# Weights that stand still in TensorE: two units worked off together, all upper products first

## The chip, the cores and the metric

The kernel runs on one core of one Trainium2 chip. What counts is the device time of one execution in microseconds (us), the median of several runs. Beside it there is one profiled execution, whose trace gives the begin and end of every instruction on every engine. The engines are TensorE (PE; its weight loads are shown apart as PEld), VectorE (DVE), ScalarE (ACT), GpSimd (POOL) and SyncE (SP), which issues most transfers (DMA) from the chip's memory.

## The reference

The program is a decoder trunk of two layers over one sequence of 256 positions, width 1024, in float32. Each layer is a feed-forward block (FFN), a mixer (a recurrent block in layer one, an attention in layer two), and a second FFN. Before layer two, keys and values are computed once.

```
def swiglu(x, w_gate, w_up, w_down):
    return (jax.nn.silu(x @ w_gate) * (x @ w_up)) @ w_down
...
    for layer in range(DEPTH):
        if layer == N_A_LAYERS:
            k, v, c = shared_kv(h, kv_norm_g, w_kv, w_fgate, b_fgate)
        f = swiglu(rms_norm(h, ffn1_pre_g[layer]), ffn1_w_gate[layer], ffn1_w_up[layer], ffn1_w_down[layer])
        h = h + 0.5 * rms_norm(f, ffn1_post_g[layer])
        ...  (mixer)
        f = swiglu(rms_norm(h, ffn2_pre_g[layer]), ffn2_w_gate[layer], ffn2_w_up[layer], ffn2_w_down[layer])
        h = h + 0.5 * rms_norm(f, ffn2_post_g[layer])
```

`w_gate` and `w_up` are 1024 x 2816, `w_down` is 2816 x 1024. There are four FFNs, so most of the weights, and most of the time, are theirs.

## The kernel before, in words

**Precision.** A float32 product is made of three products of a narrower type (fp32r). Every weight and every input is split into an upper part (rounded to fp32r) and a lower part (what is left). Upper weight times upper input, upper weight times lower input, and lower weight times upper input are added up in PSUM.

**Units.** Weights come in units of half a megabyte: 128 partitions of 1024 numbers. A unit is loaded into a tile `raw` (five buffers, by SP's queue), then ACT rounds it into `whi` (line 204) and DVE subtracts to get `wlo` (line 205); there are nine buffers of each (`WB`). The list `items` holds, in the order of use, a pair of functions for each unit: `prep` (load and split) and `work` (the products).

**Two ways to multiply.** For `w_down` and some others the input stands still in TensorE and the weights move through it (`mm3`, lines 212 to 214, products of 512 columns). For most of gate, up and the keys the weights stand still (`still`, line 518, and `mmj`, line 227). There a unit is two rows of 128 of the weight (k and k+1) by 512 columns, that is, eight blocks of 128 x 128. For each block, line 238 loads the upper weights and moves 512 columns through: the 256 upper inputs and the 256 lower inputs side by side. After these eight products, line 242 loads the lower weights and moves the 256 upper inputs only, again eight products. I call the first "upper products" and the second "lower products". Four units make a group (k from 0 to 7), which fills four of the eight PSUM banks; the next group uses the other four while ACT and DVE empty the first (line 513 adds up on ACT, line 514 on DVE, then lines 600, 601, 607, 611, 612 make the hidden values).

**Order.** PE's order is the order in which the program is written; the other engines' order is set by a scheduler from what is written. `slot` runs the next unit's `work`, counts the unit as done, and calls `tick`. `tick` is where other work is asked for: it counts down deferred functions (`defer`: transposes on PE, for instance) and runs those that are due, and it may call `prepare_next`, which asks for one more unit to be loaded and split if a model of the pace says so and the unit nine places back is done. `still` itself also calls `tick` once, after all sixteen products of the unit. So there are two ticks for each unit, both after the unit's lower products.

**The opening.** The first three units are worked off in halves, with other steps between (`hooks`: functions that bring up the next parts of the input, line 1350). Two ticks after the last of them is set, `rstd_rows` (line 298) is due: two small products on line 301 turn the row statistics into a row (`rrow`, copied out by ACT, line 303), which the first group's line 600 multiplies with. Its PSUM bank is one of those that the second group will use.

Of the kernel before, what the change touches and what calls it, by code (L numbers as in the profile page):

```python
# [16 lines left out]
P = 128  # L17
# [30 lines left out]
def trunk_kernel(ctx: ExitStack, tc: tile.TileContext, A: dict, out: bass.AP):  # L48
# [64 lines left out]
    def tick():  # L113
        for p in list(pend):
            p[0] -= 1
            if p[0] < 0 and not (p[2] and state["edge"]):
                pend.remove(p)
                p[1]()
        purse[0] = min(purse[0] + SHARE, SHARE)
        if state["p"] >= OPEN:  # L120
            prepare_next()
        while queue and purse[0] > 0:
            cost, _, fn = queue.pop(0)
            purse[0] -= cost
            fn()
# [101 lines left out]
    def mmj(bs, parts, ks, moving):  # L227

        o, oh = pall, pall[:, :, :S]
        if len(moving(ks[0])[0].shape) == 4:  # L230
            o = o.rearrange("p n (a t b) -> p n a t b", a=2, t=2)
            oh = oh.rearrange("p n (t b) -> p n t b", t=2)
        else:
            o = o.rearrange("p n (a b) -> p n a b", a=2)
        for k, (wh, wl) in zip(ks, parts):
            tensor_work(2 * S * len(bs))
            for b, w in zip(bs, wh):
                nc.tensor.matmul(o[:, b], w, moving(k)[0], start=k == 0, stop=False)  # L238
        for k, (wh, wl) in zip(ks, parts):
            tensor_work(S * len(bs))  # L240
            for b, w in zip(bs, wl):
                nc.tensor.matmul(oh[:, b], w, moving(k)[1], start=False, stop=k == 7)  # L242


    def rstd_of(ss, n, f=1.0):
# [128 lines left out]
    items = []  # L374
    units = {}
    done = {}
    state = {"p": 0, "a": 0, "b": 0, "edge": False, "look": 99}
# [23 lines left out]
    def slot(t, i):  # L401
        while state["p"] <= i:
            prepare_next(True)
        items[i][1](t, units[i])
        done[i] = done.get(i, 0) + (1 if t is not None else 2)
        if done[i] == 2:
            units.pop(i)
        tick()
# [106 lines left out]

    hooks = {}

    def still(u, k0, b0, moving=x_moving):
        if k0 == 0:
            assert not set(held) & set(range(b0, b0 + 4)), held.keys()  # L520
            lent.update(range(b0, b0 + 4))
        state["edge"] = k0 in (0, 6)
        parts = []
        for j in range(2):
            cut = [slice(j * 512 + b * P, j * 512 + b * P + P) for b in range(4)]
            parts.append(([u.hi[:, c] for c in cut], [u.lo[:, c] for c in cut]))
        if hooks:
            for j in range(2):
                if k0 + j in hooks:
                    hooks.pop(k0 + j)()  # L530
                mmj(range(b0, b0 + 4), parts[j:j + 1], [k0 + j], moving)
                if j == 0:
                    tick()
        else:
            mmj(range(b0, b0 + 4), parts, [k0, k0 + 1], moving)
            tick()
        if k0 == 6:
            lent.difference_update(range(b0, b0 + 4))
            state["edge"] = True

    def tile_items(w, c0, b0, post, moving=x_moving):
        for k0 in range(0, 8, 2):
            def prep(k0=k0):
                return split(load_raw(w[k0 * P:(k0 + 2) * P, c0:c0 + 512].rearrange("(k p) n -> p k n", p=P), P, 1024),
                             P, 1024)

            def work(t, u, k0=k0):
                still(u, k0, b0, moving)
                if k0 == 6:
                    post(b0, 4)  # L550
            items.append((prep, work))

    def ffn_items(pool_of, wg, wu, wd, post_g, next_dests, last=False, normed=False, lead=1):
        hid = {}
        sil = {}
        box = {}

        def hid_tiles():
            if not hid:
                v = hid["all"] = pool_of().tile([P, 2, 2, 22, P], F32R, tag="hid", name=nm("hid"), bufs=1)  # L560
                hid["hhi"], hid["hlo"] = v[:, 0], v[:, 1]
            return hid["hhi"], hid["hlo"]

        def gate_tile(n):
            return pool_of().tile([P, 1024], F32, tag="sil", name=nm("sil"), bufs=1)[:, :n]

        def prod_tile(n):
            return pool_of().tile([P, 16 * HA], F32, tag="prod", name=nm("prod"), bufs=1)[:, :n]

        def post_gate(t, ps):  # L570
            if t == 0:
                box["s"] = gate_tile(1024)
            s = sil[t] = box["s"][:, t * 512:(t + 1) * 512]
            nc.scalar.activation(s, ps, AF.Silu, scale=rs[t][:, 0:1])

        def post_up(c0):
            def f(t, ps):
                if t == 0:
                    box["p"] = prod_tile(1024)
                pr = box["p"][:, t * 512:(t + 1) * 512]  # L580
                nc.vector.tensor_tensor(pr, ps, sil[t], ALU.mult)
                defer(HT, lambda: hidden_T(pr, t))

            def hidden_T(pr, t):
                hh, hl = hid_tiles()
                tp = sparebank()
                for j in range(4):
                    nc.tensor.transpose(tp[:, j * P:(j + 1) * P], pr[:, j * P:(j + 1) * P], ident)
                k0 = c0 // P
                hv = hh[:, t, k0:k0 + 4, :].rearrange("p a b -> p (a b)")  # L590
                lv = hl[:, t, k0:k0 + 4, :].rearrange("p a b -> p (a b)")
                nc.scalar.activation(hv, tp, AF.Copy)
                nc.vector.tensor_tensor(lv, tp, hv.bitcast(F32), ALU.subtract)
            return f

        def gate_rows(b, m):
            s = sil["j"] = gate_tile(m * S)
            v = s.rearrange("p (a b) -> p a b", a=m)
            total(v, b, m)
            nc.vector.tensor_tensor(v, v, rcp["v"].unsqueeze(1).to_broadcast([P, m, S]), ALU.mult)  # L600
            nc.scalar.activation(s, s, AF.Silu)  # L601

        def up_rows(b, m, k0):
            pr = prod_tile(m * S)
            hh, hl = hid_tiles()
            total(pr.rearrange("p (a b) -> p a b", a=m), b, m)
            nc.vector.tensor_tensor(pr, pr, sil["j"], ALU.mult)  # L607
            pv = pr.rearrange("p (a t b) -> p a t b", a=m, t=2)
            hv = hh[:, :, k0:k0 + m, :].rearrange("p t a b -> p a t b")
            lv = hl[:, :, k0:k0 + m, :].rearrange("p t a b -> p a t b")  # L610
            nc.scalar.activation(hv, pv, AF.Copy)  # L611
            nc.vector.tensor_tensor(lv, pv, hv.bitcast(F32), ALU.subtract)

        def last_items(c0):
            for k0 in range(0, 8, 2):
                def prep(k0=k0):
                    raw = new_raw()
                    v = raw.rearrange("p (k s n) -> p k s n", k=2, s=2)
                    for s, w in enumerate((wg, wu)):
                        nc.sync.dma_start(v[:, :, s, :], w[k0 * P:(k0 + 2) * P, c0:c0 + 256].rearrange("(k p) n -> p k n", p=P))  # L620
                    return split(raw, P, 1024)

                def work(t, u, k0=k0):
                    still(u, k0, 4)
                    if k0 == 6:
                        gate_rows(4, 2)
                        up_rows(6, 2, c0 // P)
                items.append((prep, work))

        i0 = len(items)  # L630
        for i in range(5):
            if i < lead:
                proj_items(wg, i * 512, 512, main_x, post_gate)
                proj_items(wu, i * 512, 512, main_x, post_up(i * 512))
            else:
                tile_items(wg, i * 512, 4, gate_rows)
                tile_items(wu, i * 512, 0, lambda b, m, i=i: up_rows(b, m, 4 * i))
        last_items(2560)

        def load_gb():  # L640
            box["gb"] = gain_bcast(post_g)

        ahead(i0 + 24, load_gb)

        def post_down(t, accs):
            enter(t, next_dests(t, hid), accs, box["gb"], True, last, normed)

        i2 = len(items)
        row_items(wd, [P] * 22, lambda t, k: (hid["hhi"][:, t, k, :], hid["hlo"][:, t, k, :]), post_down, 4 if last else 2)
        return i0 + 8 * lead, i2, len(items)  # L650
# [625 lines left out]
    for i in range(OPEN):  # L1276
        u = units[i] = Unit()
# [165 lines left out]
```

## Time and profile before

| what | value |
|---|---|
| median of three runs | 991.96 us (991.91 to 992.14) |
| profiled execution, its own time | 991.76 us |
| its span (first to last instruction of the program) | 990.0 us |
| PE busy, PEld busy | 978.2 us, 836.3 us |
| DVE busy, ACT busy | 675.8 us, 564.2 us |
| moved from memory | 182.06 MB, 184 GB/s over the span |
| granted TensorE clock | 0.999 |

A row of the page's list of groups reads: line, engine, operation, what is written from what, shapes and count; after the bar, busy time and the mean of one in nanoseconds; after the second bar, how long the engine sat idle before such an instruction and who ended most of that. A matmul's shown time covers its whole passage through the array, and successive ones overlap, so that what a product costs is the distance from its start to the next one's start. A row of the timeline gives start and length in us, engine, line, operation, and how many instructions in a row it merges; an idle time before it stands in brackets with what ended it.

### The profile page before, as it was taken

How to read it: one execution, taken by the hardware profiler on the slowest of the kernel's cores; microseconds unless marked ns; L12 is line 12 of the kernel's file. 1: busy time of each engine (PE TensorE's matmuls, PEld its weight loads, DVE VectorE, ACT ScalarE, POOL GpSimd, SP SyncE). 2: the span in 40 equal slices, each digit the busy share in tenths (PEclk: the TensorE clock that was granted, in tenths of full speed). 3: DMA queues.
4: the chain of work that ended last, by engine and by line, in shares of the span. 5: the costliest groups of instructions: out<-in, count | busy, mean ns of one | idle time of the engine just before them, and what ended most of it. 6: DMA issues, size and time to landing. Idle time of an engine off the chain costs nothing.

```text
span 990.0 us, 13894 instructions
## 1 busy us (share of the span) xinstructions
PE 978.2 (99%) x5294; PEld 836.3 (84%) x5294; DVE 675.8 (68%) x791; ACT 564.2 (57%) x740; POOL 51.4 (5%) x97
## 2 busy tenths in 40 slices
PE   8999999999999999999999999999999999999997
PEld 6888888899978888888898888888887688888885
DVE  5877664668997776664697676674488867667542
ACT  6666543559986655543565555553467666555431
POOL 3300000100003000000000000000030000000000
PEclk9999999999999999999999999999999999999999
DMA  7887645565337766646468666654585157665431
GB/s 259 267 281 223 199 150 191 167 182 154 113 101 233 235 191 186 196 150 179 116 217 280 190 182 192 194 189 157 171 296 173 40 174 246 190 194 187 154 116 42
DMA packets 94088, 182.06 MB, mean 184 GB/s; under 512 B 11822, under 2 KB 33414, under 8 KB 93894
## 3 DMA queue, kind: packets, MB, share of 16 engines
q1 hardware_dynamic: 93350, 181.10, 58.7%
q8 instruction: 41, 0.67, 0.3%
q0 software_dynamic: 640, 0.07, 0.1%
q14 instruction: 25, 0.20, 0.1%
q10 hardware_dynamic: 32, 0.01, 0.0%
HBM read 180.09 MB, written 1.06 MB: 183 GB/s over the span
## 4 chain that ended last, share of the span: by engine, by line
PE 72%; issue 21%; DVE 3%; ACT 3%; POOL 1%; DMA 0%; DVEq 0%; POOLq 0%; SPq 0%; ACTq 0%
PE pall L238 25%; PE pall L242 13%; PE pall L212 9%; PE pall L214 9%; PE pall L213 9%; PE pall L865 1%; PE pall L219 1%; PE pall L220 1%; PE pall L221 1%; DVE wlo L205 1%; PE pall L1169 1%; PE pall L1196 1%; POOL rstd L250 1%; ACT whi L204 0%; ACT junk L255 0%
## 5 line engine op out<-in xcount | busy, mean ns | idle before, releaser
L205 DVE TENSOR_TENSOR wlo<-raw,whi 128x1024 fp32r<-128x1024 f32 (+4 forms) x328 | 393.1, 1206 | 237.5 <-ACT whi L204 236.2
L204 ACT ACTIVATE whi<-raw 128x1024 fp32r<-128x1024 f32 (+4 forms) x328 | 340.7, 1046 | 286.3 <-PE pall L214 114.4
L238 PE MATMUL pall<-xall,whi 128*128 128x512 f32 x1280 | 321.9, 393 | 1.4 <-ACT rrow L303 0.9
L238 PEld LDWEIGHTS pall<-xall,whi 128*128 128x128 f32 x1280 | 230.0, 189 | 43.2 <-ACT rrow L303 1.1
L242 PEld LDWEIGHTS pall<-xall,wlo 128*128 128x128 f32 x1280 | 174.9, 190 | 13.1 <-DVE wlo L1301 0.4
L242 PE MATMUL pall<-xall,wlo 128*128 128x256 f32 x1280 | 179.0, 282 | 0.0
L212 PE MATMUL pall<-whi,hid 128*128 128x512 f32 (+2 forms) x400 | 153.0, 382 | 0.0
L214 PE MATMUL pall<-whi,hid 128*128 128x512 f32 (+2 forms) x400 | 152.4, 381 | 0.3 <-DVE hid L278 0.3
L213 PE MATMUL pall<-wlo,hid 128*128 128x512 f32 (+2 forms) x400 | 152.4, 381 | 0.0
L214 PEld LDWEIGHTS pall<-whi,hid 128*128 128x128 f32 x400 | 75.1, 188 | 14.3 <-DVE hid L278 0.6
L213 PEld LDWEIGHTS pall<-wlo,hid 128*128 128x128 f32 x400 | 75.1, 188 | 13.6
L212 PEld LDWEIGHTS pall<-whi,hid 128*128 128x128 f32 x400 | 75.1, 188 | 13.6
L248 POOL TENSOR_SCALAR nv<-ss 128x1 f32<-128x1 f32 x24 | 10.4, 435 | 926.1 <-ACT junk L255 925.9
L212 PE MATMUL pall<-whi,xall 128*128 128x512 f32 (+2 forms) x144 | 57.2, 397 | 0.0
L214 PE MATMUL pall<-whi,xall 128*128 128x512 f32 (+2 forms) x144 | 55.2, 383 | 0.0
L213 PE MATMUL pall<-wlo,xall 128*128 128x512 f32 (+2 forms) x144 | 55.0, 382 | 0.0
L601 ACT ACTIVATE sil<-sil 128x1024 f32<-128x1024 f32 (+1 forms) x22 | 21.6, 984 | 24.7 <-DVE sil L600 24.7
L611 ACT ACTIVATE hid<-prod 128x1024 fp32r<-128x1024 f32 (+1 forms) x22 | 21.6, 984 | 19.3 <-DVE prod L607 19.3
L214 PEld LDWEIGHTS pall<-whi,xall 128*128 128x128 f32 x144 | 27.0, 188 | 5.4 <-DVE xall L278 0.3
L212 PEld LDWEIGHTS pall<-whi,xall 128*128 128x128 f32 x144 | 27.1, 188 | 4.9
L213 PEld LDWEIGHTS pall<-wlo,xall 128*128 128x128 f32 x144 | 27.1, 188 | 4.5
L318 DVE SCALAR_TENSOR_TENSOR t<-pall,rstd,gb 128x512 f32<-128x512 f32 x16 | 11.9, 748 | 26.7 <-ACT junk L255 26.7
(193 smaller groups left out, 978.7 us busy)
## 6 DMA issues: line engine op xcount, KB each, us to landing
raw<-in_ffn_w_down_dram SPq DMA_DIRECT2D x88, 512.0 KB
raw<-in_ffn_w_up_dram SPq DMA_DIRECT2D x80, 512.0 KB
raw<-in_ffn_w_gate_dram SPq DMA_DIRECT2D x78, 512.0 KB
raw<-in_rg_w_in_dram SPq DMA_DIRECT2D x20, 504.0 KB
raw<-in_ffn_w_gate_dram SPq DMA_DIRECT2D x20, 256.0 KB
raw<-in_rg_w_out_dram SPq DMA_DIRECT2D x10, 504.0 KB
raw<-in_ffn_w_up_dram SPq DMA_DIRECT2D x16, 256.0 KB
raw<-in_w_kv_dram SPq DMA_DIRECT2D x8, 512.0 KB
```

Source lines behind the costliest of these rows:

```text
L204: nc.scalar.activation(hi[:parts, c:c + m], rawv[:, c:c + m], AF.Copy)
L205: nc.vector.tensor_tensor(lo[:parts, c:c + m], rawv[:, c:c + m], hi[:parts, c:c + m].bitcast(F32), ALU.subtract)
L212: nc.tensor.matmul(ps, xh, wh, start=first, stop=False)
L213: nc.tensor.matmul(ps, xh, wl, start=False, stop=False)
L214: nc.tensor.matmul(ps, xl, wh, start=False, stop=last)
L219: nc.tensor.matmul(ps, wh, xh, start=first, stop=False)
L238: nc.tensor.matmul(o[:, b], w, moving(k)[0], start=k == 0, stop=False)
L242: nc.tensor.matmul(oh[:, b], w, moving(k)[1], start=False, stop=k == 7)
L248: nc.gpsimd.tensor_scalar(v, ss[:, 0:1], ss[:, 1:2] if n == 2 else 0.0, D * EPS * f * f, ALU.add, ALU.add)
L318: nc.vector.scalar_tensor_tensor(t1[n], pf[n], r_in, gb[:, n * 512:(n + 1) * 512], ALU.mult, ALU.mult)
L601: nc.scalar.activation(s, s, AF.Silu)
L611: nc.scalar.activation(hv, pv, AF.Copy)
```

## The change

`still` now takes a list of units. `grouped` keeps a unit back until the second of its half of the group is there (k = 0 and 2, or 4 and 6), and then works off both: 16 upper products, then 16 lower products, where before there were 8, 8, 8, 8. While `hooks` still holds steps of the opening, and for a unit left alone after that (the fourth of the first group), a unit is worked off by itself as before. The first unit's `work` of two returns at once, without the tick and without counting the unit as done; both are counted after the second.

The ticks move. With two units, `mmj` calls `tick` after the 8th and the 16th upper product and after the 8th lower product, and `slot` calls it after the last lower product: four ticks for two units, as before, but one after each eight products. With one unit, the tick that stood after the lower products now stands after the upper ones. `state["edge"]` (it holds back deferred work that is marked calm) is set for a half of the group instead of a unit.

On PE, at the opening (`whi_125` and `wlo_126` are the fourth unit's parts, `whi_127` and `wlo_128` the fifth's), before:

```order
L238 MATMUL pall<-xall,whi_125 128x512 x8
L242 MATMUL pall<-xall,wlo_126 128x256 x8
L301 MATMUL pall<-ident,rstd_221 128x128
L301 MATMUL pall<-ident,rstd_230 128x128
L238 MATMUL pall<-xall,whi_127 128x512 x8
L242 MATMUL pall<-xall,wlo_128 128x256 x8
L238 MATMUL pall<-xall,whi_276 128x512 x8
L242 MATMUL pall<-xall,wlo_277 128x256 x8
```

and now, where the lines 238, 242 and 301 have become 239, 245 and 306 and the sixth unit's parts are called `whi_268` and `wlo_269`:

```order
L239 MATMUL pall<-xall,whi_125 128x512 x8
L306 MATMUL pall<-ident,rstd_221 128x128
L306 MATMUL pall<-ident,rstd_230 128x128
L245 MATMUL pall<-xall,wlo_126 128x256 x8
L239 MATMUL pall<-xall,whi_127 128x512 x8
L239 MATMUL pall<-xall,whi_268 128x512 x8
L245 MATMUL pall<-xall,wlo_128 128x256 x8
L245 MATMUL pall<-xall,wlo_269 128x256 x8
```

The two products of `rstd_rows` have moved from behind the fourth unit's lower products to ahead of them, and the fifth and sixth units are the first two that go together.

On ACT at the same place, before (`junk` are the row statistics, `whi_127` is the fifth unit, `sil_280` the first group's sum, which can begin when the fourth unit's lower products are done):

```order
L255 ACTIVATE junk_226,ss_225<-h 128x1024
L1297 ACTIVATE whi_127<-raw_109 128x1024
L513 ACTIVATE sil_280<-pall 128x1024
L303 ACTIVATE rrow_272<-pall 128x256
L204 ACTIVATE whi_276<-raw_274 128x1024
L204 ACTIVATE whi_303<-raw_301 128x1024
```

and now (513 has become 519, 303 has become 308, 1297 has become 1321):

```order
L260 ACTIVATE junk_226,ss_225<-h 128x1024
L1321 ACTIVATE whi_127<-raw_109 128x1024
L308 ACTIVATE rrow_264<-pall 128x256
L204 ACTIVATE whi_268<-raw_266 128x1024
L519 ACTIVATE sil_280<-pall 128x1024
L204 ACTIVATE whi_295<-raw_293 128x1024
```

The copy of the row and the sixth unit's upper part now stand ahead of the first group's sum.

On PE at the first two units of the second FFN that stand still (`whi_2937` and `whi_3048`; line 588's are transposes of the hidden values of the columns before), before:

```order
L214 MATMUL pall<-whi_2904,xall 128x512
L238 MATMUL pall<-xall,whi_2937 128x512 x8
L242 MATMUL pall<-xall,wlo_2938 128x256 x8
L588 MATMUL pall<-ident,prod_3058 128x128 x4
L238 MATMUL pall<-xall,whi_3048 128x512 x8
L242 MATMUL pall<-xall,wlo_3049 128x256 x8
```

and now (line 588 has become 611):

```order
L214 MATMUL pall<-whi_2904,xall 128x512
L239 MATMUL pall<-xall,whi_2937 128x512 x8
L239 MATMUL pall<-xall,whi_3048 128x512 x8
L611 MATMUL pall<-ident,prod_3058 128x128 x4
L245 MATMUL pall<-xall,wlo_2938 128x256 x8
L245 MATMUL pall<-xall,wlo_3049 128x256 x8
```

The four transposes now stand behind sixteen upper products instead of behind eight upper and eight lower ones. Away from the units that stand still (the projections, the recurrent block, the down products, the attention) PE's order is as before. On POOL nothing is moved, and on SP one transfer of weights changes place with three small ones in the first FFN.

```diff
     def mmj(bs, parts, ks, moving):
...
-        for k, (wh, wl) in zip(ks, parts):
+        n = len(ks)
+        for i, (k, (wh, wl)) in enumerate(zip(ks, parts)):
             tensor_work(2 * S * len(bs))
             for b, w in zip(bs, wh):
                 nc.tensor.matmul(o[:, b], w, moving(k)[0], start=k == 0, stop=False)
-        for k, (wh, wl) in zip(ks, parts):
+            if n > 1 and i % 2 == 1:
+                tick()
+        for i, (k, (wh, wl)) in enumerate(zip(ks, parts)):
             tensor_work(S * len(bs))
             for b, w in zip(bs, wl):
                 nc.tensor.matmul(oh[:, b], w, moving(k)[1], start=False, stop=k == 7)
+            if i == 1 and n > 2:
+                tick()
...
     def slot(t, i):
         while state["p"] <= i:
             prepare_next(True)
-        items[i][1](t, units[i])
+        if items[i][1](t, units[i]):
+            return
         done[i] = done.get(i, 0) + (1 if t is not None else 2)
...
-    def still(u, k0, b0, moving=x_moving):
+    def still(us, k0, b0, moving=x_moving):
         if k0 == 0:
             assert not set(held) & set(range(b0, b0 + 4)), held.keys()
             lent.update(range(b0, b0 + 4))
+        n = 2 * len(us)
         state["edge"] = k0 in (0, 6)
         parts = []
...
+        run_ = 1 if hooks else n
+        for j in range(0, n, run_):
+            if k0 + j in hooks:
+                hooks.pop(k0 + j)()
+            mmj(range(b0, b0 + 4), parts[j:j + run_], range(k0 + j, k0 + j + run_), moving)
+            if run_ == 1 and j == 0:
+                tick()
+        if k0 + n == 8:
             lent.difference_update(range(b0, b0 + 4))
-            state["edge"] = True
+        state["edge"] = k0 + n == 8
+
+    def grouped(k0, kept, fn):
+
+        i = len(items)
+
+        def work(t, u):
+            kept.append((i, u))
+            if len(kept) < 2 and not hooks and k0 % 4 == 0:
+                return [i]
+            us = [v for _, v in kept]
+            done_ = [j for j, _ in kept]
+            del kept[:]
+            fn(us, k0 + 2 - 2 * len(us))
+            for j in done_[:-1]:
+                done[j] = 2
+                units.pop(j)
+        return work
...
-            def work(t, u, k0=k0):
-                still(u, k0, b0, moving)
+            def go(us, k, k0=k0):
+                still(us, k, b0, moving)
                 if k0 == 6:
                     post(b0, 4)
-            items.append((prep, work))
+            items.append((prep, grouped(k0, kept, go)))
```

The last group of each FFN (half gate, half up columns) is changed in the same way.

More of the change, by code (lines that the diff above doesn't have):

```diff
@@ L521, in still @@
             lent.update(range(b0, b0 + 4))
+        n = 2 * len(us)
         state["edge"] = k0 in (0, 6)
         parts = []
[L524 to L527, printed above, removed]
+        for u in us:
             for j in range(2):
[L529 to L537, printed above, removed]
-            lent.difference_update(range(b0, b0 + 4))
-            state["edge"] = True
+                cut = [slice(j * 512 + b * P, j * 512 + b * P + P) for b in range(4)]
+                parts.append(([u.hi[:, c] for c in cut], [u.lo[:, c] for c in cut]))
+        run_ = 1 if hooks else n
[6 more added lines that the diff above has]
+        if k0 + n == 8:
+            lent.difference_update(range(b0, b0 + 4))
+        state["edge"] = k0 + n == 8
[13 more added lines that the diff above has]
+        return work
     def tile_items(w, c0, b0, post, moving=x_moving):
+        kept = []
         for k0 in range(0, 8, 2):
@@ L614, in last_items @@
         def last_items(c0):
+            kept = []
             for k0 in range(0, 8, 2):
@@ L621, in prep, with go @@
                     return split(raw, P, 1024)
-                def work(t, u, k0=k0):
-                    still(u, k0, 4)
+                def go(us, k, k0=k0):
+                    still(us, k, 4)
                     if k0 == 6:
@@ L627, in work @@
                         up_rows(6, 2, c0 // P)
-                items.append((prep, work))
+                items.append((prep, grouped(k0, kept, go)))
         i0 = len(items)
```

## The prediction

> **What bounds the kernel now.** I read the page's busy times, the chain that ended last and the groups first:
>
> ```profile
> span 990.0 us, 13894 instructions
> PE 978.2 (99%) x5294; PEld 836.3 (84%) x5294; DVE 675.8 (68%) x791; ACT 564.2 (57%) x740; POOL 51.4 (5%) x97
> PE 72%; issue 21%; DVE 3%; ACT 3%; POOL 1%; DMA 0%; DVEq 0%; POOLq 0%; SPq 0%; ACTq 0%
> L238 PE MATMUL pall<-xall,whi 128*128 128x512 f32 x1280 | 321.9, 393 | 1.4 <-ACT rrow L303 0.9
> L242 PE MATMUL pall<-xall,wlo 128*128 128x256 f32 x1280 | 179.0, 282 | 0.0
> ```
>
> PE is busy in 99% of the span and sits idle before lines 238 and 242 for 1.4 us in all. "Busy" doesn't say that each product is as fast as it can be, so I went to the starts of products next, in the timeline of PE alone. First a stretch of units, then products of 512 columns with nothing else between them (the down products), then products of 256 columns inside one run:
>
> ```profile
> 402.36 2.00 PE L238 MATMUL pall<-xall,whi 128*128 128x512 f32 x8
> 404.20 1.12 PE L242 MATMUL pall<-xall,wlo 128*128 128x256 f32 x8
> ...
> 338.11 0.40 PE L238 MATMUL pall<-xall,whi 128*128 128x512 f32 x1
> 430.29 1.09 PE L238 MATMUL pall<-xall,whi 128*128 128x512 f32 x4
> ...
> 440.14 0.39 PE L213 MATMUL pall<-wlo,hid 128*128 128x512 f32 x1
> 470.06 0.39 PE L213 MATMUL pall<-wlo,hid 128*128 128x512 f32 x1
> ...
> 404.31 0.52 PE L242 MATMUL pall<-xall,wlo 128*128 128x256 f32 x3
> 404.91 0.40 PE L242 MATMUL pall<-xall,wlo 128*128 128x256 f32 x2
> ```
>
> Between 338.11 and 430.29 lie 33 units: 92.18 / 33 = 2.7933 us each. Between the two rows of line 213 lie 44 rounds of lines 212 to 214, 132 products: 29.92 / 132 = 0.2267 us from start to start. Inside the lower run five products take 0.60 us: 0.120 each. Eight and eight at these distances would be 8 x 0.2267 + 8 x 0.120 = 2.773 us. A unit takes 2.793. So **a unit pays 20 ns more than its products cost in long runs**. Where it is paid, the next rows show: a run of upper products that follows no lower ones (the first after a projection), and one that follows only four lower ones (the opening).
>
> ```profile
> 332.11 1.98 PE L238 MATMUL pall<-xall,whi 128*128 128x512 f32 x8
> 333.93 1.11 PE L242 MATMUL pall<-xall,wlo 128*128 128x256 f32 x8
> ...
> 15.97 0.63 PE L242 MATMUL pall<-xall,wlo 128*128 128x256 f32 x4
> 16.45 2.02 PE L238 MATMUL pall<-xall,whi 128*128 128x512 f32 x8
> 18.30 1.11 PE L242 MATMUL pall<-xall,wlo 128*128 128x256 f32 x8
> ```
>
> After a projection eight upper products take 1.82 us (8 x 0.2267 = 1.81); after eight lower ones 1.84 (402.36 to 404.20); after four lower ones 1.85. The surplus is paid by upper products that follow lower ones, and it is as large after four as after eight: a price of the switch, not of the number of lower products.
>
> Last, what units wait for (the view of line 238), and what ACT and DVE wait for:
>
> ```profile
> L238 PE MATMUL pall<-hid,whi x64: 387/389/481, 518.8 to 540.6; 128*128 128x512 f32 x64
> its engine sat idle before it (us, times) until:
>   ACT rrow L303: 2.1, 2
>   DVE xall L1293: 1.4, 2
> ...
> DVE wlo L205 <- ACT whi L204: 236.2, 174, 5.7
> ACT whi L204 <- PE pall L238: 97.1, 73, 1.8
> ```
>
> No upper product ever waited for weights; ACT, which cuts them, waits for PE to give a buffer back. So supply runs ahead as far as nine buffers allow. PE is the bound, and the only wait before units in the long run is that for `rrow`, at the opening.
>
> **The change, part by part.**
>
> *The switches.* The x1280 and x64 rows give 1344 upper products, 168 units. The first four go alone; 164 go in 82 pairs. A pair has one switch from lower to upper where two units had two, and everything else is the same instructions. So 82 x 20 ns = **1.64 us less**, all on the path, as PE waits for nothing there. The ends: nothing gained, if the surplus comes with every eight products or grows with the run; and 3.6 us, if lower products behind the eighth came at 0.117 us, as the nearest long run of 256 columns has them:
>
> ```profile
> 264.14 0.28 PE L220 MATMUL pall<-xall,whi 128*84 128x256 f32 x1
> 264.96 0.28 PE L221 MATMUL pall<-xall,wlo 128*84 128x256 f32 x1
> ```
>
> (seven starts in 0.82 us; 82 x 8 x 3 ns = 2.0 more). Those weights are narrower; the row of the same shape has 0.120, so I stay with 20 ns.
>
> *The opening.* `rstd_rows` moves ahead of the fourth unit's lower products, and ACT's copy of `rrow` ahead of the first group's sum. Before:
>
> ```profile
> 16.93 1.04 ACT L1297 ACTIVATE whi<-raw 128x1024 fp32r<-128x1024 f32 x1
> 17.79 0.58 POOL L250 TENSOR_TENSOR rstd<-nv,mhalf 128x1 f32<-128x1 f32 x1
> 19.25 0.61 PE L301 MATMUL pall<-ident,rstd 128*128 128x128 f32 x4
> 19.45 1.02 ACT L513 ACTIVATE sil<-pall 128x1024 f32<-128x1024 f32 x1 [1.47 <-PE pall L242]
> 20.37 0.38 ACT L303 ACTIVATE rrow<-pall 128x256 f32<-128x256 f32 x1
> 20.63 2.96 ACT L204 ACTIVATE whi<-raw 128x1024 fp32r<-128x1024 f32 x3
> 20.80 2.14 PE L238 MATMUL pall<-xall,whi 128*128 128x512 f32 x8 [0.94 <-ACT rrow L303]
> ```
>
> Line 301 writes into a bank that the fifth unit needs; its copy stood behind the sum (19.45 to 20.37), so PE idled until 20.80. From 16.45 to 20.80 are 4.35 us. Now: upper products to 18.30, line 301 for 0.44 (four starts, of which the row shows (0.61 - 0.27) / 3 = 0.11 each), lower products 0.95: 3.24 us, the fifth unit at 19.69. The statistics must be there: POOL ends the second at 18.37, and the second pair of line 301 is due at 18.52. The copy must be out in time: line 301 ends at 18.30 + 0.61 = 18.91, ACT is free since 17.97, the copy ends at 19.29, 0.4 us ahead of need. So **1.1 us less**; at worst nothing, if the statistics come so late that all of it is lost; at best 0.1 more, as the row's eight products took 1.97 (20.80 to 22.77, where the lower ones begin) after the wait.
>
> What is late next there: the sixth unit's upper part is needed in the pair's second eight, at about 19.69 + 1.85 = 21.54. ACT begins it after the copy, at 19.3, as it now stands ahead of the sum, so it ends at 20.4; even at the old 20.63 + 1.06 = 21.69 PE would lose 0.15.
>
> *Transposes and other inserted products.* They are the same, but four stand now ahead of lower products instead of upper ones. One that stays ahead of upper products shows the price of interrupting:
>
> ```profile
> 40.56 0.25 PE L162 MATMUL pall<-ident,grow 40*128 40x40 f32 x1
> 40.74 2.11 PE L238 MATMUL pall<-xall,whi 128*128 128x512 f32 x8
> 42.69 1.12 PE L242 MATMUL pall<-xall,wlo 128*128 128x256 f32 x8
> ```
>
> The run takes 1.95 instead of 1.84: 0.11 us. Ahead of lower products it may be between 0 and 0.22; four times that difference is 0.4 us either way. I take 0, the middle.
>
> *Buffers and the other engines.* A pair's first unit needs its lower part 1.8 us later, its second unit its upper part 0.95 us earlier; both counted against a supply that waits for buffers. The lower buffer of the first unit is given back 1.8 us later, so DVE's subtraction nine units on waits longer and holds up what stands behind it. DVE has room:
>
> ```profile
> 540.00:660.00 120.00, 120.00 (x690) 105.60 (x689) 82.85 (x71) 65.35 (x64) 0.00 (x0) 1.00 0.63 188
> ```
>
> 82.85 of 120 us (third busy number) and a PSUM bank that isn't needed again for 11 us (four units): I take 0. The same four ticks per pair cost nothing, as they are only places in the program. The other stages keep their order, so their waits move along.
>
> **The sum.** 1.64 + 1.1 = 2.7 us off the profiled execution's span: 990.0 to 987.3, with its own time 991.76 to 989.0. The median of the runs is 0.2 above that execution: 991.96 - 2.7 = **989.2 us**, 0.28% less. I call "same" what lies within 0.2% (2.0 us), about what a measurement here can tell from no change.
>
> **The rivals.**
>
> *The switch isn't what costs.* If the 20 ns belong to every eight products, or double with the run, the pairs gain nothing and only the opening is left: 991.96 - 1.1 = 990.9, same. The equal 1.84 and 1.85 speak against it; that no run of 16 is in the trace speaks for leaving it open. The Trainium skill, page "TensorE: Matmul & The Clock Gate", section "Back-to-back issue gap", comes out here too: it gives the distance between products from the number of columns alone (N / 2.4 + 2.5 ns, which I work out to 216 and 109 ns), so that their order would be worth nothing. The trace differs in both figures (227 and 120) and has the surplus. Chance 0.12.
>
> *The opening isn't won.* If PE waits for the statistics or for the sixth unit by as much as it waited for `rrow`, only the switches are left: 990.3, same. POOL's 18.37 against 18.52 is close, but a miss costs the miss alone, not 1.1. Chance 0.10.
>
> *Lower buffers held too long (slower).* DVE works in order. Per pair (5.57 us) it is busy 0.69 x 5.57 = 3.85 us; add 1.8 in which it may now stand before a buffer that isn't free, and it needs 5.65, 0.08 more than PE. PE would then be paced by DVE: 82 x 0.08 = 6.6 slower, less 2.7: 995.9. It decides only once the supply has been used up, and a DVE that falls behind finds its buffers free, which ends the standing. Chance 0.06.
>
> **How the numbers follow.** Forecast as worked out, 0.67 (own range 988.5 to 989.9); the two cases of half a gain, 0.22; slower, 0.06; another partial loss that leaves the time within 0.2%, 0.05. Faster 0.68, same 0.26, slower 0.06. The range goes down by 0.8 to 988.4 (0.4 for the inserted products, 0.1 for the opening, 0.3 of the 2.0 for faster lower products) and up to 991.0, just past the case of the opening alone.
>
> **What would show it.** Sixteen upper products from start to the first lower one in 3.65 us (1.84 + 8 x 0.2267), sixteen lower ones in 1.91, a pair in 5.57 where two units took 5.59. The wait for `rrow` gone, the fifth unit's first product near 19.7 us. No upper product that waits for `whi`, no lower one for `wlo`. I am wrong if a pair takes 5.59 or more, or if PE shows idle time before line 239 or 245 in the middle of an FFN.

## The result, and the profile after

The changed kernel takes 989.35 us (median of 11 runs, 988.85 to 989.97) against 991.75 us for the one before (11 runs, 991.58 to 992.14), a ratio of 0.9975 with a 95% interval of 0.9966 to 0.9984. That is 2.4 us less, where 2.7 were forecast. The page of the changed kernel, and what its line 239 and DVE waited for:

```profile
span 987.9 us, 13888 instructions
PE 976.8 (99%) x5294; PEld 837.2 (85%) x5294; DVE 672.7 (68%) x791; ACT 567.3 (57%) x740; POOL 50.7 (5%) x97
L239 PE MATMUL pall<-xall,whi 128*128 128x512 f32 x1280 | 307.2, 392 | 0.4 <-DVE xall L1317 0.4
L245 PE MATMUL pall<-xall,wlo 128*128 128x256 f32 x1280 | 167.2, 283 | 0.0
...
PEld pall L239 <- DVE xall L1317: 0.8, 1, 0.8
PEld pall L239 <- DVE par L744: 0.4, 1, 0.4
...
DVE wlo L205 <- ACT whi L204: 113.5, 82, 5.7
DVE wlo L205 <- issue: 94.5, 37, 3.2
...
DVE wlo L205 <- PE pall L245: 30.1, 34, 2.4
```

The copy of `rrow` is no longer among those that PE waits for. There is a new wait, 0.4 us for `par` (the recurrent block's parameters, line 744), and DVE now does stand before lower buffers that PE has not given back. The profile names PE for 30.1 us in 34 waits, and "issue" (nothing that it shows) for another 94.5 us in 37; by the starts and ends in the trace the two are of one kind, since DVE begins 93 to 95 ns after the eighth lower product of a pair, the last that reads the first unit's lower part, in each of the 71. Together they are 124.6 us. No product of lines 239 and 245 waits for `whi` or `wlo`.

The timeline of PE in the long run, and at the opening, there with POOL's and ACT's rows:

```profile
401.96 2.08 PE L245 MATMUL pall<-xall,wlo 128*128 128x256 f32 x16
403.87 3.82 PE L239 MATMUL pall<-xall,whi 128*128 128x512 f32 x16
407.53 2.08 PE L245 MATMUL pall<-xall,wlo 128*128 128x256 f32 x16
409.44 2.91 PE L239 MATMUL pall<-xall,whi 128*128 128x512 f32 x12
...
16.70 2.00 PE L239 MATMUL pall<-xall,whi 128*128 128x512 f32 x8
17.54 0.58 POOL L255 TENSOR_TENSOR rstd<-nv,mhalf 128x1 f32<-128x1 f32 x1
18.54 0.61 PE L306 MATMUL pall<-ident,rstd 128*128 128x128 f32 x4
18.90 1.20 PE L245 MATMUL pall<-xall,wlo 128*128 128x256 f32 x8
19.18 0.38 ACT L308 ACTIVATE rrow<-pall 128x256 f32<-128x256 f32 x1 [1.30 <-PE pall L306]
19.46 1.05 ACT L204 ACTIVATE whi<-raw 128x1024 fp32r<-128x1024 f32 x1
19.94 0.86 PE L239 MATMUL pall<-xall,whi 128*128 128x512 f32 x3
```

A pair goes from 403.87 to 409.44, 5.57 us: 3.66 for the upper products, 1.91 for the lower ones. At the opening the fifth unit begins 19.94 - 16.70 = 3.24 us after the fourth, where it was 4.35.

To see where the rest went, I cut each trace into the same pieces: from the first upper product to the fourth unit, from there to the fifth, from there to the first down product, and the three later stretches in which weights stand still (second FFN of layer one; keys and first FFN of layer two; second FFN of layer two), from their first upper product to the first product of the down weights. "Rest" is the span without these pieces and without the time ahead of the first upper product. All in us, each from starts of products in one trace:

| kernel | to unit 4 | 4 to 5 | 5 to end of first FFN | second | third | fourth | rest |
|---|---|---|---|---|---|---|---|
| before | 10.12 | 4.35 | 112.33 | 100.97 | 145.79 | 100.97 | 509.18 |
| changed | 9.81 | 3.24 | 112.15 | 100.62 | 145.35 | 100.62 | 509.23 |
| opening alone | 9.87 | 3.25 | 112.21 | 100.97 | 145.83 | 100.97 | 509.16 |
| pairs alone | 10.43 | 4.34 | 112.29 | 100.62 | 145.35 | 100.62 | 509.18 |
| ticks last | 10.09 | 3.24 | 112.23 | 100.61 | 145.29 | 100.61 | 509.47 |
| halves | 9.97 | 3.71 | 112.75 | 101.23 | 146.89 | 101.23 | 509.23 |
| second pair turned | 10.11 | 3.25 | 111.69 | 100.47 | 145.05 | 100.47 | 509.10 |
| four together | 9.78 | 3.24 | 111.61 | 100.47 | 145.09 | 100.47 | 509.23 |
| parameters later | 10.18 | 3.27 | 111.83 | 100.62 | 145.35 | 100.62 | 509.14 |
| changed again | 9.79 | 3.25 | 112.15 | 100.62 | 145.35 | 100.62 | 509.12 |
| four together, parameters later | 9.78 | 3.24 | 111.61 | 100.47 | 145.09 | 100.47 | 509.25 |

The first column varies between 9.8 and 10.4 though nothing in it was moved; the changed kernel itself has 9.81 and 9.79. In the profiled execution of the changed kernel the first upper product also came 0.56 us later (6.89 against 6.33). The change's own pieces are the others: 1.11 (opening), 0.19, 0.35, 0.45 and 0.35, together 2.45 us, close to the 2.40 of the medians. (The two profiled spans differ by 2.1 us only, because of that later first product.)

### The profile page after: what moved, and what is told of

Same layout as the page of the kernel before. It is cut to its first block, busy times and chain, and to the rows that moved or that the text cites. A ratio compares the mean times of both kernels' runs of the same rounds, so it can differ in the third digit from the quotient of the medians.

```text
span 987.9 us, 13888 instructions
## 1 busy us (share of the span) xinstructions
PE 976.8 (99%) x5294; PEld 837.2 (85%) x5294; DVE 672.7 (68%) x791; ACT 567.3 (57%) x740; POOL 50.7 (5%) x97
## 3 DMA queue, kind: packets, MB, share of 16 engines
HBM read 180.09 MB, written 1.06 MB: 183 GB/s over the span
## 4 chain that ended last, share of the span: by engine, by line
PE 72%; issue 21%; ACT 3%; DVE 3%; POOL 1%; DMA 0%; DVEq 0%; POOLq 0%; ACTq 0%
PE pall L239 25%; PE pall L245 13%; PE pall L212 9%; PE pall L214 9%; PE pall L213 9%; PE pall L889 1%; PE pall L219 1%; PE pall L220 1%; PE pall L221 1%; DVE wlo L205 1%; PE pall L1193 1%; PE pall L1220 1%; POOL rstd L255 1%; ACT whi L204 0%; ACT junk L260 0%
## 5 line engine op out<-in xcount | busy, mean ns | idle before, releaser
L205 DVE TENSOR_TENSOR wlo<-raw,whi 128x1024 fp32r<-128x1024 f32 (+4 forms) x328 | 388.9, 1206 | 238.9 <-ACT whi L204 113.5
L239 PE MATMUL pall<-xall,whi 128*128 128x512 f32 x1280 | 307.2, 392 | 0.4 <-DVE xall L1317 0.4
L239 PEld LDWEIGHTS pall<-xall,whi 128*128 128x128 f32 x1280 | 235.1, 188 | 46.2 <-DVE xall L1317 0.8
L245 PEld LDWEIGHTS pall<-xall,wlo 128*128 128x128 f32 x1280 | 164.6, 191 | 6.5
L245 PE MATMUL pall<-xall,wlo 128*128 128x256 f32 x1280 | 167.2, 283 | 0.0
L519 ACT ACTIVATE prod<-pall 128x1024 f32<-128x1024 f32 (+1 forms) x22 | 20.8, 948 | 18.4 <-PE pall L245 18.4
L519 ACT ACTIVATE sil<-pall 128x1024 f32<-128x1024 f32 (+1 forms) x22 | 20.9, 949 | 18.3 <-PE pall L245 18.3
```

What stands on the lines that cost most here:

```text
L205: nc.vector.tensor_tensor(lo[:parts, c:c + m], rawv[:, c:c + m], hi[:parts, c:c + m].bitcast(F32), ALU.subtract)
L519: nc.scalar.activation(v, pall[:, b:b + m, S:], AF.Copy)
```

## The experiments

**The opening alone.** No two units together; a single unit's tick stands after its upper products, as in the changed kernel.

```diff
             kept.append((i, u))
-            if len(kept) < 2 and not hooks and k0 % 4 == 0:
-                return [i]
```

> No two units go together; only the tick of a unit stands after its upper products, as in the changed kernel, so that the two products of the row of statistics and its copy keep their new place at the opening. My theory (opening 1.1 us, switches 1.64 us, independent of each other): 1.1 us less than before, a unit in the long run still 2.793 us, the fifth unit begins 3.24 us after the fourth one's first upper product instead of 4.35. The rival that the whole gain comes from working in pairs: no gain here.

Measured: 990.43 us (11 runs) against 991.68 (33 runs of the kernel before), ratio 0.9987 (0.9978 to 0.9996): 1.25 us less. Rows of its timeline, and as the last one a row of the kernel before:

```profile
16.39 2.02 PE L239 MATMUL pall<-xall,whi 128*128 128x512 f32 x8
18.24 0.61 PE L306 MATMUL pall<-ident,rstd 128*128 128x128 f32 x4
18.61 1.20 PE L245 MATMUL pall<-xall,wlo 128*128 128x256 f32 x8
19.64 2.00 PE L239 MATMUL pall<-xall,whi 128*128 128x512 f32 x8
21.48 1.12 PE L245 MATMUL pall<-xall,wlo 128*128 128x256 f32 x8
...
22.77 1.10 PE L242 MATMUL pall<-xall,wlo 128*128 128x256 f32 x8
```

From 16.39 to 19.64 are 3.25 us, and the second and fourth stretch are as long as before (100.97). The 1.1 us of the opening are won without any pair. So are another 0.12 us in the piece behind it (112.21 against 112.33): the fifth unit's upper products take 1.84 us (19.64 to 21.48), where behind the wait for `rrow` they took 1.97 (20.80 to 22.77).

**The pairs alone.** Two units together, but a single unit's tick is back behind its lower products.

```diff
-            if n > 1 and i % 2 == 1:
+            if n > 2 and i % 2 == 1:
                 tick()
...
-            if i == 1 and n > 2:
+            if i == 1 and n > 1:
                 tick()
```

> Two units go together, but the fourth unit keeps its tick behind its lower products, so that the opening is as before. My theory: 1.64 us less than before, a pair in 5.567 us, the wait for the row's copy as before (4.35 us from the fourth unit's start to the fifth's). The rival that the switch costs nothing and only the opening won: no gain here.

Measured: 990.47 us against 991.68, ratio 0.9988 (0.9979 to 0.9997): 1.21 us less, where 1.64 were expected. The stretches two to four are those of the changed kernel to a hundredth, so the switches bring the same without the new opening; with 18 pairs in the second and in the fourth, 0.353 us / 18 = 19.6 ns a pair. At the opening the wait is back:

```profile
18.47 1.11 PE L245 MATMUL pall<-xall,wlo 128*128 128x256 f32 x8
20.54 0.38 ACT L308 ACTIVATE rrow<-pall 128x256 f32<-128x256 f32 x1
20.80 2.96 ACT L204 ACTIVATE whi<-raw 128x1024 fp32r<-128x1024 f32 x3
20.97 3.96 PE L239 MATMUL pall<-xall,whi 128*128 128x512 f32 x16 [0.94 <-ACT rrow L308]
24.77 0.40 PE L245 MATMUL pall<-xall,wlo 128*128 128x256 f32 x2
```

PE waits 0.94 us for `rrow` as before. The sixteen upper products then take 3.80 us instead of 3.65. That is the aftermath of the wait: the first product's successor starts 341 ns behind it instead of 233, and the slow ones after it are more than usual. The kernel before pays nearly the same behind its wait (1.97 us instead of 1.84 for eight), so this takes next to nothing from the gain. The sixth unit's upper part, begun at 20.80 (1.06 each), ends near 21.9 and is due at about 22.9, so it isn't late. The missing part lies in the first FFN, which is 0.04 us shorter where 20 pairs at 20 ns should save 0.40, and to a small part in the third stretch (0.45 where 26 pairs should save 0.52). This kernel too waits 0.4 us for `par` in the first FFN; what that costs is shown below. The opening alone and the pairs alone add up to 2.46 us; the changed kernel has 2.40.

**Ticks at the end of the pair.** The changed kernel, but the three ticks inside a pair come together after its last product.

```diff
-            if i == 1 and n > 2:
-                tick()
...
             if run_ == 1 and j == 0:
                 tick()
+            if run_ == 4:
+                for _ in range(3):
+                    tick()
```

(and the tick after upper products stays for a single unit only.)

> The changed kernel, but the three ticks inside a pair all come at the pair's end instead of after each eight products. My theory holds the even distances for worth nothing, since supply stands nine buffers ahead: 2.7 us less than before, like the changed kernel, within 0.4. The rival, that the even distances carry part of the gain: less than 2 us gained, with upper products that wait for weights, or with transposes that are waited for.

Measured: 989.47 us against 991.68, ratio 0.9978 (0.9969 to 0.9987): 2.21 us less. The second to fourth stretch are those of the changed kernel or shorter by up to 0.06; the first FFN behind the opening is 0.08 longer and the rest 0.24. The even distances of the other work are worth at most that, and nothing that these runs can tell.

**Halves.** The other direction: four upper, four lower products, twice as many switches as before.

```diff
-        run_ = 1 if hooks else n
+        run_ = 1
```

(and no two units together, as in the first experiment.)

> The other way: units are worked off in halves, four upper products and four lower ones, so that there are twice as many switches as before. The unit in the opening that already goes so takes 1.40 us for a half, 2.80 for a unit, because four upper products after a switch cannot pay what the fifth would pay: 164 x 7 ns = 1.1 us more, less 1.1 us for the opening, so the time of before within 0.5 us, and a unit of 2.80 us in the trace. If each switch cost its full 20 ns whatever its run, a unit would take 2.813 us and the time would be 2.2 us over before. If the surplus went with the number of products alone, a unit would take 2.793 us as before, and the time would be 1.1 us under it.

Measured: 993.04 us against 991.68, ratio 1.0012 (1.0003 to 1.0021): 1.36 us more. I had expected the time of before within 0.5, so this was a miss, and both of its terms were off. At the opening only 0.64 us are won (3.71 against 4.35), because line 306 now comes before the statistics (0.84 us from its first product to the next upper one, where the opening alone has 0.37 to the next lower one):

```profile
17.89 0.38 PE L306 MATMUL pall<-ident,rstd 128*128 128x128 f32 x2
18.48 0.49 PE L306 MATMUL pall<-ident,rstd 128*128 128x128 f32 x2 [0.21 <-POOL rstd L255]
18.73 1.17 PE L239 MATMUL pall<-xall,whi 128*128 128x512 f32 x4
```

In the long run the second and fourth stretch have the expected 7 ns a unit (0.25 us / 36), but the third has 1.10 us / 52 = 21 ns a unit, its inserted products among them: there every other half takes 1406 ns instead of 1400. Why it does so in that stretch (and in the first) and not in the others, I did not find out. Against the opening alone, which has no wait for `rrow` either, the extra 164 switches cost 0.53 + 0.25 + 1.06 + 0.25 = 2.1 us over all four, 13 ns each: more switches cost more, on average less than 20 ns where runs are of four.

**The second pair turned.** Pairs go upper, lower, then lower, upper: one switch from lower to upper less for each group.

```diff
+        swap = n == 4 and ks[0] == 4
+        for f in (lower, upper) if swap else (upper, lower):
+            f()
```

(`upper` and `lower` are the two loops of `mmj` as functions, with the same four ticks for two units.)

> The changed kernel, but the second pair of each group goes the other way round, its sixteen lower products first, so that a group has one switch from lower to upper less (32 lower products in a row inside a group, and upper products next to upper products between groups). My theory, a price of 20 ns for each switch: 41 groups x 20 ns = 0.82 us less than the changed kernel, 3.5 us less than before, a group in 11.11 us instead of 11.13. The rival, a surplus that grows with the run: the changed kernel's time, 2.7 us less than before.

Measured: 988.31 us (5 runs) against 991.74 (9 runs), ratio 0.9965 (0.9952 to 0.9977): 3.43 us less.

```profile
401.77 3.52 PE L249 MATMUL pall<-xall,wlo 128*128 128x256 f32 x28
405.13 7.44 PE L241 MATMUL pall<-xall,whi 128*128 128x512 f32 x32
412.41 4.00 PE L249 MATMUL pall<-xall,wlo 128*128 128x256 f32 x32
416.25 4.04 PE L241 MATMUL pall<-xall,whi 128*128 128x512 f32 x17
```

From 405.13 to 416.25 a round of 64 products takes 11.12 us; two pairs take 11.13 (by the medians over the whole traces 11.114 and 11.134). The second and fourth stretch are 0.15 us shorter than the changed kernel's, 17 ns for each of nine groups. The surplus does not double with a run of 32. This trace has no wait for `par` (the wait of the changed kernel, taken up below), so the first FFN's 0.46 us over the changed kernel are mostly that wait; without its 0.32 us the four pieces are 0.73 us shorter, 18 ns for each of 41 groups.

**Four together.** All upper products of a group, then all lower ones.

```diff
-            if len(kept) < 2 and not hooks and k0 % 4 == 0:
+            if k0 < 6 and not hooks:
                 return [i]
```

(with a tick after each eight products here too, and calm work let in after the first sixteen.)

> All four units of a group together, 32 upper products and then 32 lower ones. By the price of the switch alone 0.82 us less than the changed kernel, 3.5 us less than before. It also holds the buffers longer: the first unit's lower buffer is given back after 40 products instead of 24. The rival of the buffers held too long expects PE to wait for weights and the time to be above the changed kernel's; my theory has the supply two units shorter, still several units ahead, and no wait, except perhaps at the opening, where the sixth to eighth unit's upper parts are asked for up to 2.9 us earlier than with single units.

Measured: 988.09 us (5 runs) against 991.74, ratio 0.9963 (0.9949 to 0.9977): 3.65 us less. The stretches are as with the second pair turned. What DVE waited for:

```profile
DVE wlo L205 <- ACT whi L204: 120.5, 82, 5.7
DVE wlo L205 <- PE pall L247: 90.8, 35, 4.1
```

DVE stands for 90.8 us before lower buffers not yet given back, up to 4.1 us at a time (95.0 us with one more such wait put down to "issue"). That is less in all than the changed kernel's 124.6, in half as many waits. The products of lines 239 and 247 still never wait for a weight. The rival of the buffers held too long has its mechanism in the trace, but no price.

**The parameters later.** The one new wait of the changed kernel, for `par`, follows the transpose of the parameters (line 743), which now stands just ahead of the last eight lower products before a new group:

```profile
74.11 1.11 PE L245 MATMUL pall<-xall,wlo 128*128 128x256 f32 x8
75.07 0.24 PE L743 MATMUL pall<-ident,prow 88*126 88x88 f32 x1
75.10 1.20 PE L245 MATMUL pall<-xall,wlo 128*128 128x256 f32 x8
76.13 1.13 PE L239 MATMUL pall<-xall,whi 128*128 128x512 f32 x3
...
76.47 0.24 DVE L744 COPY par<-pall 126x88 f32<-126x88 f32 x1
```

Its result lies in a PSUM bank that the group beginning at 76.13 needs, and DVE copies it only at 76.47. One number puts it back where it stood before:

```diff
-    defer(40, rg_params, True)
+    defer(44, rg_params, True)
```

> The changed kernel with one number changed: the transpose of the recurrent block's parameters is due 44 ticks after it is asked for instead of 40, and so stands again where it stood before, behind the lower products of the pair with wlo_679, and not between the lower products of the pair ahead of it, just before a new group takes its PSUM bank. My reading of the changed kernel's trace is that PE waits there 0.4 us for DVE's copy of the parameters: that wait gone, the first stage 0.2 to 0.3 us shorter in the trace. If the lost part of the first stage has another cause, its length stays.

```profile
79.68 2.08 PE L245 MATMUL pall<-xall,wlo 128*128 128x256 f32 x16
81.59 0.24 PE L743 MATMUL pall<-ident,prow 88*126 88x88 f32 x1
81.62 3.66 PE L239 MATMUL pall<-xall,whi 128*128 128x512 f32 x15
```

Measured: 989.11 us (6 runs) against 991.78 (14 runs), ratio 0.9971 (0.996 to 0.9983). The wait is gone, and the piece from the fifth unit to the end of the first FFN is 111.83 instead of 112.15: 0.32 us shorter, a little more than expected. The medians cannot tell 0.15 us from the changed kernel's, which was run beside it:

> The changed kernel as it is, once more, beside the others of this job: 2.4 us less than before; the stages of units that stand still as long as in its first trace, within 0.1 us but for the opening.

Measured: 989.26 us (9 runs) against 991.78, ratio 0.9974 (0.9965 to 0.9984): 2.5 us less; every piece of its trace but the rest within 0.03 us of the first one's, the rest 0.10 shorter.

**Four together, parameters later.** The kernel with four together and `defer(46, rg_params, True)`.

> All four units of a group together, with that transpose 46 ticks after it is asked for, in a group's lower products ahead of three more units' lower products, so that the bank is free again in time. By the price of the switch 0.8 us less than the changed kernel, and 0.2 to 0.3 us for the wait: about 1.1 us less than the changed kernel, 3.5 us less than before.

Measured: 988.21 us (5 runs) against 991.78, ratio 0.9965 (0.9951 to 0.9979): 3.6 us less, 1.05 less than the changed kernel run beside it. The part of the expectation about the wait was wrong: in the trace with four together and the transpose at its 40 ticks there is no wait for `par`, and its pieces are the same with 46 (111.61 both). What the first FFN gained over pairs (0.54 us) holds the 0.32 of that wait and 0.22 for ten groups, 22 ns each.

## Why the prediction was right

*The switches* were the main term, 82 x 20 ns = 1.64 us. The price of a pair came out at 19.6 ns in the second and the fourth stretch, where nothing else was moved but four transposes, and the run of sixteen continues as the long runs did: 3.66 and 1.91 us, where 3.65 and 1.91 stood in the forecast. The third stretch gave 0.45 us for 26 pairs (17 ns each). The first FFN shows only 0.19 for 20, but there three things are mixed: 0.12 us that belong to the opening, 0.32 lost to the wait for `par`, and the pairs. The opening alone (112.213) and the parameters later (111.827) have the same opening and neither has that wait; between them the 20 pairs bring 0.39 us, 19 ns each. So 1.54 of the 1.64 us are there.

*The opening* was forecast to bring the fifth unit 3.24 us after the fourth; the trace has 3.24, and the opening alone shows that it doesn't need the pairs. With the 0.12 us that the fifth unit's products no longer lose behind a wait, which the forecast had only as its best case, the opening is worth 1.23 us instead of 1.1. POOL's statistics ended at 18.12, 0.6 us ahead of the products that need them, where the forecast had 0.15. That much room was luck: the same margin is 0.24 us in the opening alone, 0.15 with the second pair turned and 0.12 with the parameters later. The halves, where line 306 came half a unit sooner, show where that margin ends (0.21 us of waiting).

*Inserted products* were set to 0, between ends of 0.4 us either way. This is the term that was mis-sized: 0.32 us were lost to it, though not by the mechanism I had put there (the interruption of a run). One transpose came to stand so close ahead of the next group that its bank was not emptied in time. The ordered program showed where that transpose had gone; I looked at what it interrupts, not at what waits for its bank. Idle time before line 239 in the middle of an FFN was one of my signs of being wrong, and here it did show, once, on the weight loads (PEld): 0.4 us.

*Buffers and the other engines* at 0: right, with DVE's standing seen (124.6 us, and 95.0 with four together) and nothing of it on PE's path. DVE sat idle before line 205 for 237.5 us before and 238.9 now: it stands before PE's buffers where it used to wait for ACT. Supply was never used up, so what such a standing would cost then stays open.

The sum: 1.64 + 1.1 = 2.74 forecast; 1.54 + 1.23 - 0.32 = 2.45 in the trace's pieces, 2.40 in the medians. That the time itself came as close as 989.35 to 989.2 is in part luck: the forecast took 0.3 us too much off a median of three runs that lay 0.2 above that of eleven. One slip of the forecast changes nothing: its four cases add up to 0.67 for faster and 0.27 for same, not 0.68 and 0.26.

The rival that the switch isn't what costs fell with the pairs alone and with the two kernels of one switch a group. By the Trainium skill's formula in "TensorE: Matmul & The Clock Gate", section "Back-to-back issue gap", which the page gives for an isolated product and in which only the number of columns counts, none of the three could have gained by its order. The traces differ from it: all three gained (19.6 ns a pair, and 17 more a group, in the second stretch). The rival that the opening isn't won fell with the opening alone.

## What to carry to other kernels

Where PE is busy in 99% of the span, compare what a round of work takes with what its products take in long runs of their own kind: the difference (here 20 ns of 2793) is the most that another order of the same instructions can win in a round, and counting the switches that it removes gives the gain where nothing else moves (here 0.35 us for 18 pairs). When a step is moved, follow the buffer it writes as well as the work it interrupts: the next user of its PSUM bank may now come too soon. And a copy that frees a bank for PE should not stand in its engine's queue behind work that can wait.

## What the runs showed of the hardware

The 20 ns are not one gap. In the trace of before, the eight upper products after lower ones start 233, 236, 228, 232, 231, 227, 227, 227 ns apart (medians by place in the run); from the sixth on, and through all of a run of 16, it is 226 to 227; and the first lower product after upper ones costs 113 instead of 120. Only the first five after a switch are slow. A run of four pays less for its switch than a run of eight: in the second stretch of the halves, four and four take 1.400 us where 4 x 0.2267 + 4 x 0.120 = 1.387 would be due, 13 ns more; the slower halves of 1406 pay 19. What delays them was not measured, nor which of the differences between upper and lower products (columns moved, weights, place in PSUM) makes the switch. Before the change nothing in the page hinted at this: PE was shown busy throughout.
